# A float32 decoder trunk on one core: each 512-column product as two runs of 256 columns in one PSUM bank

## The chip, the core and the metric

The kernel runs on one core of one Trainium2 chip. The metric is the device time of one execution in microseconds; the number that counts is the median over several runs.

## The reference

One layer of a hybrid decoder on 2048 tokens of width 1024, in float32, with 16 learned tokens put in front and dropped at the end:

```
h = concat(meta, x)                                # 2064 x 1024
u = rmsnorm(h);  p = u @ w_in                      # 1024 -> 1792
y = concat(pool(p_a), conv31(p_b), rglru(p_c))     # three causal mixers
h = h + y @ w_out                                  # 1024 -> 1024
u = rmsnorm(h)
h = h + square(relu(u @ w_up)) @ w_down            # 1024 -> 4096 -> 1024
out = rmsnorm(h)[16:]
```

The four big products (w_in, w_out, w_up, w_down) are nearly all of the arithmetic. The mixers add moving averages, a depthwise convolution of 31 taps with a layer norm, a gated linear recurrence, and small products of their own.

## The kernel before

**Layout.** Activations lie channel-major, [channel, token]: 128 channels on the partitions, tokens along the columns. The tokens are worked off in four chunks of 512 (the first has the 16 extra tokens and 528 columns).

**Products.** Every float32 operand is split into a high part and the rest (`split`, lines 87 and 88: ScalarE writes the high part, VectorE the rest). A product adds hi*hi, hi*lo and lo*hi. One *item* is one block of 128 output channels for one chunk: `mm_tile` (line 178) runs over eight blocks k of 128 input channels and three split products each, that is 24 matmuls of 512 columns that add up in one PSUM bank (a tile `pm`, five of them). In the first chunk the inner projections have two sub-ranges of 264 columns in two banks, 48 matmuls an item. The instruction is recorded at line 184.

**The tiles.** The token side of a product is a list of eight split tiles [128, 2, columns]. Tiles with the tag `U` (eight of 2 x 512 columns, from `a_tile`) hold the input of later chunks' projections and the hidden values between the up and the down product. Tiles with the tag `H` (eight of 2 x 528, from `b_tile`) hold the first chunk's input, the mixers' output (for w_out) and the normed input of the up product. Weights are streamed: a DMA brings 128 x 1024 values (tag `wr`, three tiles), and two splits make two tiles `wh` of 4 blocks k each (five tiles in all). A weight block is split at most one item ahead.

**Items and their order.** They are listed by hand: W (input projection, 14 items a chunk), O (w_out, 8), U (up, 8 for each of four groups g) and D (down, 8 for each group). A chunk's mlp is U, D, U, D and so on: eight U items give the eight hidden tiles which the next eight D items read. `evac_u` (line 626) makes a hidden tile out of a U item's bank: relu and square on ScalarE (630, 632), a cast and a subtraction on VectorE (633, 634). `evac_d` adds a D item's bank to the residual (639). In the last group of the last chunk the D items are done in two halves of 256 tokens, each half with its weights streamed anew, so that the final norm of the first half can begin early.

**What runs beside them.** Behind every item `pump` issues pieces of other work (the next chunk's mixers, norms and splits) up to a budget of estimated nanoseconds; the scheduler of the language may place an instruction that is ready ahead of one that still waits, and so small matmuls of the mixers (tag `pb`) stand among those of the items.

Of the kernel before, what the change touches and what calls it, by code (L numbers as in the profile page):

```python
"""Hybrid decoder trunk: pool / conformer-conv / RG-LRU mixers and a squared-ReLU MLP on one core.

Activations are held channel-major, [channel, token], in four chunks of 512 tokens.  Every
matrix product splits both float32 operands exactly into a 12-bit high part and the 12-bit
rest, and adds the three products hi*hi, hi*lo and lo*hi in float32.
"""
# [12 lines left out]
P = 128  # L19
D = 1024  # L20
KB = D // P
NT = 512
NCH = 4
META = 16
W0 = NT + META
# [9 lines left out]
BUD1 = 2000  # L35
GELU_C = 0.7978845608028654

# packed per-channel vectors: name -> (first column, columns)
_VECS = [
    ("g1", 8), ("g2", 8), ("gf", 8), ("psc", 2), ("lam", 4), ("ba", 4), ("bx", 4),  # L40
    ("rcb", 4), ("cb", 2), ("lng", 2), ("lnb", 2), ("rcw", 16), ("cw", 62),
# [5 lines left out]
    _o += _c  # L47
NVEC = _o

# projection blocks in the order they are computed: (kind, index, weight block)  # L50
_WORDER = (
    [("bv", 0, 2), ("bg", 0, 4), ("bv", 1, 3), ("bg", 1, 5)]
    + [("cx", i, 10 + i) for i in range(4)]
# [5 lines left out]
def build(nc, tc, x0, xr, w_in, w_out, w_up, w_down, vecs, gates, pools, pws, out):  # L59
    V = nc.vector  # L60
    A = nc.scalar
    T = nc.tensor
# [24 lines left out]
        A.activation(out=hi, in_=src, func=AF.Copy)  # L87
        V.tensor_tensor(out=lo, in0=src, in1=hi.bitcast(F32), op=ALU.subtract)  # L88

# [1 line left out]
    vec = t_("vec", NVEC, 1)  # L91
    nc.sync.dma_start(out=vec, in_=vecs)

# [18 lines left out]
    def load_consts():  # L112
        for name, src, cols in (("gw", gates, 1024), ("pw", pws, 512), ("pl", pools, 256)):
            raw = t_("wr", 1024, 3)
            nc.sync.dma_start(out=raw[:, :cols], in_=src)
            hl = t_("c_" + name, (2, cols), 1, F32R)
            split(hl[:, 0, :], hl[:, 1, :], raw[:, :cols])
            cst[name] = hl
            yield 1500
        # csp = 8 * softplus(-lam)  # L120
        lam = vr("lam")
        s = t_("sp", (8, 4), 1)
        al, e, den, w, w2, q, m = (s[:, i, :] for i in range(7))
        V.tensor_scalar(out=al, in0=lam, scalar1=-1.0, scalar2=None, op0=ALU.mult)
        V.tensor_scalar(out=m, in0=al, scalar1=0.0, scalar2=None, op0=ALU.max)
        V.tensor_tensor(out=al, in0=al, in1=lam, op=ALU.max)
        A.activation(out=e, in_=al, func=AF.Exp, scale=-1.0)
        V.tensor_scalar(out=den, in0=e, scalar1=2.0, scalar2=None, op0=ALU.add)
        V.reciprocal(den, den)
        V.tensor_tensor(out=w, in0=e, in1=den, op=ALU.mult)  # L130
        V.tensor_tensor(out=w2, in0=w, in1=w, op=ALU.mult)
        NTERM = 10
        V.tensor_scalar(out=q, in0=w2, scalar1=1.0 / (2 * NTERM + 1), scalar2=1.0 / (2 * NTERM - 1), op0=ALU.mult, op1=ALU.add)
        for i in range(NTERM - 2, -1, -1):
            V.tensor_tensor(out=q, in0=q, in1=w2, op=ALU.mult)
            V.tensor_scalar(out=q, in0=q, scalar1=1.0 / (2 * i + 1), scalar2=None, op0=ALU.add)
        V.tensor_tensor(out=q, in0=q, in1=w, op=ALU.mult)
        V.scalar_tensor_tensor(out=q, in0=q, scalar=2.0, in1=m, op0=ALU.mult, op1=ALU.add)
        csp = t_("csp", (2, 4), 1)
        V.tensor_scalar(out=csp[:, 0, :], in0=q, scalar1=-8.0, scalar2=None, op0=ALU.mult)  # L140
        V.tensor_scalar(out=csp[:, 1, :], in0=q, scalar1=4.0, scalar2=None, op0=ALU.mult)
        cst["csp"] = csp
        yield 2500
# [3 lines left out]
    tail_x = [t_(f"tlx{i}", 3, 1) for i in range(4)]  # L147
    state = [t_(f"st{i}", 1, 1) for i in range(4)]

# [1 line left out]
    class Weights:  # L151
        def __init__(self, srcs):
            self.srcs = srcs
# [22 lines left out]
                self.ns += 1  # L176

    def mm_tile(w, rhs, subs):
        """Sum over KB blocks of w-block^T @ rhs-block; rhs: list of [P, 2, cols] split tiles."""
        pss = [ps_main() for _ in subs]  # L180
        for k in range(KB):
            for j, (a, b) in enumerate(((0, 0), (0, 1), (1, 0))):
                for ps, (s0, s1) in zip(pss, subs):
                    T.matmul(  # L184
                        ps[:, : s1 - s0], w[k // 4][:, a, (k % 4) * P : (k % 4 + 1) * P], rhs[k][:, b, s0:s1],
                        start=(k == 0 and j == 0), stop=(k == KB - 1 and j == 2),
                    )
        return pss

    def mm3(ps, pairs, first=True, last=True):  # L190
        """ps = sum of split products; pairs: (w hi, w lo, rhs hi, rhs lo)."""
        n = len(pairs)
        for q, (wh, wl, rh, rl) in enumerate(pairs):
            T.matmul(ps, wh, rh, start=(first and q == 0), stop=False)  # L194
            T.matmul(ps, wh, rl, start=False, stop=False)  # L195
            T.matmul(ps, wl, rh, start=False, stop=(last and q == n - 1))  # L196
# [6 lines left out]
        return hi, lo  # L203

    def colsum(src):
        """Sum over the partitions, on every partition."""
        n = src.shape[-1]
        hi, lo = split_new(src)
        ps = ps_back()
        T.matmul(ps[:, :n], ones, hi, start=True, stop=False)  # L210
        T.matmul(ps[:, :n], ones, lo, start=False, stop=True)  # L211
        return ps

    def rsqrt_of(pss, bounds, scale):
        """1/sqrt(scale * ps + eps)"""
        rs = t_("rs", W0, 2)
        for ps, (c0, c1) in zip(pss, bounds):
            A.activation(out=rs[:, c0:c1], in_=ps[:, : c1 - c0], func=AF.Sqrt, bias=eps, scale=scale)  # L218
        c0, c1 = bounds[0][0], bounds[-1][1]
        V.reciprocal(rs[:, c0:c1], rs[:, c0:c1])  # L220
        return rs
# [6 lines left out]
            A.activation(out=sq[:, c0:c1], in_=src, func=AF.Square)  # L228
            V.tensor_tensor(out=ss[:, c0:c1], in0=ss[:, c0:c1], in1=sq[:, c0:c1], op=ALU.add)  # L229

# [1 line left out]
    class Chunk:  # L232
        pass

# [21 lines left out]
        return t_("H", (2, W0), 8, F32R)  # L256

    def gen_x0(o):
        """The first chunk: gain and split, then 1/rms with its sums over channels on the tensor engine."""
        o.x = []  # L260
        tw = o.tw
        raws = []
        for k in range(KB):
            raw = t_("xr", W0, 3) if k < 3 else t_("t", W0, TB)
            nc.sync.dma_start(out=raw, in_=x0[k])
            raws.append(raw)
            if k == 0:
                wts.dma(1)
        for k in range(KB):
            hl = b_tile()  # L270
            if k == 0:
                wts.split(1)
            A.activation(out=hl[:, 0, :], in_=raws[k], func=AF.Copy, scale=vc("g1", k))
            V.scalar_tensor_tensor(out=hl[:, 1, :], in0=raws[k], scalar=vc("g1", k), in1=hl[:, 0, :].bitcast(F32), op0=ALU.mult, op1=ALU.subtract)
            o.x.append(hl)
        yield 0
        pss = [ps_back() for _ in subs_of(o)]
        for k in range(KB):
            sq = t_("m", W0, 2)
            A.activation(out=sq, in_=raws[k], func=AF.Square)  # L280
            for ps, (s0, s1) in zip(pss, subs_of(o)):
                T.matmul(ps[:, : s1 - s0], ones.bitcast(F32), sq[:, s0:s1], start=(k == 0), stop=(k == KB - 1))  # L282
        o.rs1 = rsqrt_of(pss, subs_of(o), 1.0 / D)
        yield 0

    def gen_x(o):
        """A later chunk: gain, split and, except for the second, 1/rms."""
        o.x = []
        if o.c > 1:
            ss = t_("ss", W0, 2)  # L290
# [12 lines left out]
            yield 3500  # L303

    def gen_late(o):
        """1/rms of a chunk whose projections were stored as they came, and their scaling by it."""
        ss = t_("ss", W0, 2)
        for k in range(KB):
            raw = t_("xr", W0, 3)
# [73 lines left out]
                V.tensor_copy(tail_a[i], t[:, NT:W0])  # L383
            o.done.add(("ua", i))

# [1 line left out]
    def gen_pool(o, b):  # L387
        u = o.ua[b]
        lo_half, up_half = slice(0, 64), slice(64, 128)
        # s2[:, j] = u[j] + u[j-1], s4 the sum of four, and so on  # L390
        s2 = t_("s", W0, SBF)
        V.tensor_tensor(out=s2[:, 1:W0], in0=u[:, 1:W0], in1=u[:, 0 : W0 - 1], op=ALU.add)
        yield 620
# [65 lines left out]
    def gen_rg(o, i):  # L459
# [18 lines left out]
        yield 620  # L478
        csp = cst["csp"]
        a = t_("t", W0, TB)  # L480
        # a = exp(-x), s = tanh(x/2): 1 - a = (1 + a) s, sqrt(1 - a^2) = (1 + a) sqrt(s)
        A.activation(out=a[:, R], in_=r[:, R], func=AF.Exp, scale=csp[:, 0, i : i + 1])
        s = r
        A.activation(out=s[:, R], in_=r[:, R], func=AF.Tanh, scale=csp[:, 1, i : i + 1])
# [33 lines left out]
        yield 670  # L518

    class Lane:  # L520
        """Generators run one after the other, each as soon as what it reads is there."""

        def __init__(self, todo):
            self.todo = todo
# [20 lines left out]
    class Mix:  # L545
# [17 lines left out]
            self.turn = 0  # L563

        def step(self):
            """One piece of work; None when nothing is ready."""
            pat = PAT0 if self.o.c == 0 else PAT1
            want = pat[self.turn % len(pat)]
            if not self.lanes[-1].empty() and self.o.c == 1:
# [24 lines left out]
            o.u[k] = hl  # L594
            yield 620

# [1 line left out]
    def htile(o, j):  # L598
        if o.c == NCH - 1 and j >= 4:
            return t_("Pcx", 531, 4)  # L600
# [50 lines left out]
            nc.sync.dma_start(out=out[o.c, k, :, s0:s1], in_=h)  # L651
            yield 660

# [1 line left out]
    urgent = []  # L655
    mixes = []

# [144 lines left out]


def _blockdiag(w):
    """[heads, 64, 64] -> [128, heads/2, 128], two heads on each diagonal, zeros elsewhere."""
    n = w.shape[0] // 2
    r = np.zeros((P, n, P), w.dtype)
    for i in range(n):
        r[:64, i, :64] = w[2 * i]
        r[64:, i, 64:] = w[2 * i + 1]  # L810
    return r
# [60 lines left out]
```

## Time and profile before

| | |
|---|---|
| median of 3 runs | 2005.9 us (2004.64, 2005.90, 2006.65) |
| profiled execution, first to last instruction | 2002.8 us |
| TensorE matmuls | busy 1983.2 us (99%), 8952 instructions |
| TensorE weight loads | busy 1615.8 us (81%), 8952 instructions |
| VectorE | busy 1305.1 us (65%) |
| ScalarE | busy 925.4 us (46%) |
| HBM | 104 GB/s over the span |

For the profiled execution the span is its own time: no other figure of it is given, and what lies between span and device time (start and end) is only seen as the distance to the runs. Matmul rows overlap their neighbours, so busy time says little of the pace; the distance from start to start does.

### The profile page before, as it was taken

How to read it: one execution, taken by the hardware profiler on the slowest of the kernel's cores; microseconds unless marked ns; L12 is line 12 of the kernel's file. 1: busy time of each engine (PE TensorE's matmuls, PEld its weight loads, DVE VectorE, ACT ScalarE, POOL GpSimd, SP SyncE). 2: the span in 40 equal slices, each digit the busy share in tenths (PEclk: the TensorE clock that was granted, in tenths of full speed). 3: DMA queues.
4: the chain of work that ended last, by engine and by line, in shares of the span. 5: the costliest groups of instructions: out<-in, count | busy, mean ns of one | idle time of the engine just before them, and what ended most of it. 6: DMA issues, size and time to landing. Idle time of an engine off the chain costs nothing.

```text
span 2002.8 us, 23381 instructions
## 1 busy us (share of the span) xinstructions
PE 1983.2 (99%) x8952; PEld 1615.8 (81%) x8952; DVE 1305.1 (65%) x2092; ACT 925.4 (46%) x1510; POOL 0.2 (0%) x4
## 2 busy tenths in 40 slices
PE   8999999999999999999999999999999999999997
PEld 8987888888887788888888778888888888888887
DVE  8985799746458996555445999645635484343447
ACT  6755544654445436446343544634624343323244
POOL 0000000000000000000000000000000000000000
PEclk9999999999999999999999999999999999999999
DMA  6113432222226222222223622222222333222234
GB/s 216 43 43 104 142 102 95 95 85 95 85 94 221 95 95 85 95 95 84 95 86 104 211 95 94 85 95 95 82 97 95 121 107 125 94 95 94 94 97 148
DMA packets 66065, 209.15 MB, mean 104 GB/s; under 512 B 7456, under 2 KB 9632, under 8 KB 65952
## 3 DMA queue, kind: packets, MB, share of 16 engines
q1 hardware_dynamic: 65952, 207.65, 31.7%
q8 instruction: 70, 1.15, 0.2%
q14 instruction: 43, 0.35, 0.1%
HBM read 199.23 MB, written 8.39 MB: 104 GB/s over the span
## 4 chain that ended last, share of the span: by engine, by line
PE 95%; DVE 3%; ACT 1%; DMA 1%; issue 0%; SPq 0%; DVEq 0%; ACTq 0%
PE pm L184 92%; PE pb L194 1%; PE pb L195 1%; DVE h L650 1%; PE pb L196 1%; DMA xr<-d_xr 1%; DVE wh L88 1%; DVE rs L220 1%; PE pb L282 0%; DVE ss L229 0%; PE pb L210 0%; DMA xr<-d_x 0%; PE pb L211 0%; DVE h L610 0%; DVE Pcx L650 0%
## 5 line engine op out<-in xcount | busy, mean ns | idle before, releaser
L184 PE MATMUL pm<-H,wh 128*128 128x512 f32 (+1 forms) x4416 | 983.7, 382 | 6.3 <-ACT wh L87 6.2
L184 PE MATMUL pm<-U,wh 128*128 128x512 f32 (+1 forms) x4272 | 961.7, 384 | 0.7 <-DVE wh L88 0.7
L184 PEld LDWEIGHTS pm<-H,wh 128*128 128x128 f32 x4416 | 800.0, 188 | 179.4 <-ACT wh L87 6.2
L184 PEld LDWEIGHTS pm<-U,wh 128*128 128x128 f32 x4272 | 772.7, 188 | 179.1 <-DVE wh L88 1.8
L87 ACT ACTIVATE wh<-wr 128x512 fp32r<-128x512 f32 x684 | 429.9, 629 | 730.6 <-PE pm L184 716.5
L88 DVE TENSOR_TENSOR wh<-wr,wh 128x512 fp32r<-128x512 f32 x684 | 468.2, 689 | 445.8 <-ACT wh L87 444.0
L630 ACT ACTIVATE m<-pm 128x512 f32<-128x512 f32 x128 | 76.4, 597 | 226.0 <-PE pm L184 223.7
L639 DVE TENSOR_TENSOR h<-h,pm 128x512 f32<-128x512 f32 (+1 forms) x116 | 77.4, 667 | 112.1 <-PE pm L184 111.7
L424 DVE SCALAR_TENSOR_TENSOR ca<-Pbv,vec,ca 128x512 f32<-128x512 f32 x180 | 125.9, 744 | 0.1
L634 DVE TENSOR_TENSOR U<-m,U 128x512 fp32r<-128x512 f32 x128 | 88.2, 689 | 3.0
L632 ACT ACTIVATE m<-m 128x512 f32<-128x512 f32 x128 | 79.6, 622 | 0.0
L220 DVE RECIPROCAL rs<-rs 128x512 f32<-128x512 f32 (+2 forms) x17 | 53.9, 3169 | 14.4 <-ACT rs L218 14.3
L229 DVE TENSOR_TENSOR ss<-ss,m 128x512 f32<-128x512 f32 (+1 forms) x84 | 53.8, 642 | 6.3 <-ACT m L228 5.2
L633 DVE CAST U<-m 128x512 fp32r<-128x512 f32 x128 | 53.5, 418 | 0.1
L424 DVE SCALAR_TENSOR_TENSOR ca<-h,vec,ca 128x512 f32<-128x512 f32 x60 | 42.9, 745 | 0.1
L228 ACT ACTIVATE m<-h 128x512 f32<-128x512 f32 (+1 forms) x51 | 30.9, 605 | 9.4 <-DVE h L639 3.6
L610 DVE TENSOR_TENSOR h<-pm,xr 128x512 f32<-128x512 f32 x28 | 19.1, 684 | 19.8 <-PE pm L184 19.5
L466 DVE SCALAR_TENSOR_TENSOR t<-Pcx,vec,t 128x512 f32<-128x512 f32 x36 | 26.8, 744 | 0.8 <-ACT t L464 0.6
L477 ACT ACTIVATE t<-pb,vec 128x512 f32<-128x512 f32 (+1 forms) x40 | 22.3, 603 | 8.6 <-PE pb L196 8.3
L639 DVE TENSOR_TENSOR Pcx<-Pcx,pm 128x512 f32<-128x512 f32 (+1 forms) x20 | 11.6, 581 | 19.5 <-PE pm L184 19.5
L88 DVE TENSOR_TENSOR H<-s,H 128x512 fp32r<-128x512 f32 x32 | 20.9, 686 | 1.5 <-ACT H L87 1.3
L487 ACT ACT_TABLE_LOAD x16 | 20.5, 1283 | 0.3
(183 smaller groups left out, 810.8 us busy)
## 6 DMA issues: line engine op xcount, KB each, us to landing
wr<-d_w_down SPq DMA_DIRECT2D x136, 512.0 KB, 3.5
wr<-d_w_up SPq DMA_DIRECT2D x128, 512.0 KB, 3.5
wr<-d_w_in SPq DMA_DIRECT2D x46, 512.0 KB, 3.6
wr<-d_w_out SPq DMA_DIRECT2D x32, 512.0 KB, 3.5
xr<-d_xr SPq DMA_DIRECT2D x56, 256.0 KB, 3.3
d_out<-h SPq DMA_DIRECT2D x24, 256.0 KB, 3.0
xr<-d_x SPq DMA_DIRECT2D x8, 256.0 KB, 3.0
t<-d_x SPq DMA_DIRECT2D x5, 264.0 KB, 5.8
```

What stands on the lines that cost most here:

```text
L87: A.activation(out=hi, in_=src, func=AF.Copy)
L88: V.tensor_tensor(out=lo, in0=src, in1=hi.bitcast(F32), op=ALU.subtract)
L184: T.matmul(ps[:, : s1 - s0], w[k // 4][:, a, (k % 4) * P : (k % 4 + 1) * P], rhs[k][:, b, s0:s1], start=(k == 0 and j == 0), stop=(k == KB ...
L220: V.reciprocal(rs[:, c0:c1], rs[:, c0:c1])
L228: A.activation(out=sq[:, c0:c1], in_=src, func=AF.Square)
L229: V.tensor_tensor(out=ss[:, c0:c1], in0=ss[:, c0:c1], in1=sq[:, c0:c1], op=ALU.add)
L424: V.scalar_tensor_tensor(out=a, in0=o.ub[i][:, k : k + NT], scalar=vc("cw", i * CONVK + k), in1=a, op0=ALU.mult, op1=ALU.add)
L630: A.activation(out=r, in_=ps, func=AF.Relu)
L632: A.activation(out=r, in_=r, func=AF.Square)
L633: V.tensor_copy(hl[:, 0, :], r)
L634: V.tensor_tensor(out=hl[:, 1, :], in0=r, in1=hl[:, 0, :].bitcast(F32), op=ALU.subtract)
L639: V.tensor_tensor(out=h, in0=h, in1=ps[:, : s1 - s0], op=ALU.add)
```

## The change

`mm_tile` gets a second way for items with one sub-range, which is all but the two-bank items of the first chunk. It cuts the columns in pieces of 256 and does all 24 matmuls of the first piece, then all 24 of the second. The two pieces lie side by side in the same PSUM tile, so it is read out once, by the same instructions as before, when both are complete. An item of 512 columns has 48 matmuls and 48 weight loads; an item of 256 columns (the halves at the end) has one piece and is as it was. Nothing else is changed; the rest of the diff takes comments out.

```diff
+HALF = 256
...
     def mm_tile(w, rhs, subs):
         pss = [ps_main() for _ in subs]
+
+        def mm(ps, d0, k, a, b, s0, s1, j):
+            T.matmul(
+                ps[:, d0 : d0 + s1 - s0], w[k // 4][:, a, (k % 4) * P : (k % 4 + 1) * P], rhs[k][:, b, s0:s1],
+                start=(k == 0 and j == 0), stop=(k == KB - 1 and j == 2),
+            )
+
+        prods = ((0, 0), (0, 1), (1, 0))
+        if len(subs) == 1:
+            (ps,), ((s0, s1),) = pss, subs
+            for h0 in range(s0, s1, HALF):
+                for k in range(KB):
+                    for j, (a, b) in enumerate(prods):
+                        mm(ps, h0 - s0, k, a, b, h0, min(h0 + HALF, s1), j)
+            return pss
         for k in range(KB):
-            for j, (a, b) in enumerate(((0, 0), (0, 1), (1, 0))):
+            for j, (a, b) in enumerate(prods):
                 for ps, (s0, s1) in zip(pss, subs):
-                    T.matmul(
-                        ps[:, : s1 - s0], w[k // 4][:, a, (k % 4) * P : (k % 4 + 1) * P], rhs[k][:, b, s0:s1],
-                        start=(k == 0 and j == 0), stop=(k == KB - 1 and j == 2),
-                    )
+                    mm(ps, 0, k, a, b, s0, s1, j)
         return pss
```

## The prediction

> **What bounds the kernel now.** I read the page first: engines, chain, costliest groups.
>
> ```profile
> span 2002.8 us, 23381 instructions
> PE 1983.2 (99%) x8952; PEld 1615.8 (81%) x8952; DVE 1305.1 (65%) x2092; ACT 925.4 (46%) x1510; POOL 0.2 (0%) x4
> PE 95%; DVE 3%; ACT 1%; DMA 1%; issue 0%; SPq 0%; DVEq 0%; ACTq 0%
> L87 ACT ACTIVATE wh<-wr 128x512 fp32r<-128x512 f32 x684 | 429.9, 629 | 730.6 <-PE pm L184 716.5
> ```
>
> TensorE is the chain: 95% of the end is matmul time, and it hardly ever stands still. So the question is what one matmul costs in the stream. "Mean ns of one" cannot say that, because neighbouring matmuls overlap; the starts can. The second view groups the matmuls of the big products by shape, and gives the counts:
>
> ```profile
> L184 PE MATMUL pm<-H,wh 128*128 128x512 f32 x3936 | 919.2, 393 | 0.0
> L184 PE MATMUL pm<-U,wh 128*128 128x512 f32 x3888 | 916.9, 395 | 0.5 <-DVE wh L88 0.5
> L184 PE MATMUL pm<-H,wh 128*128 128x264 f32 x480 | 64.5, 290 | 6.3 <-ACT wh L87 6.2
> L184 PE MATMUL pm<-U,wh 128*128 128x256 f32 x384 | 44.8, 277 | 0.2 <-DVE wh L88 0.2
> ```
>
> The last row matters most: the last group of down products of the last chunk is already worked off in 256-column halves. The third view is TensorE's timeline (start, length, count) around it:
>
> ```profile
> 1678.40 44.96 PE L184 MATMUL pm<-U,wh 128*128 128x512 f32 x192
> 1723.20 44.53 PE L184 MATMUL pm<-H,wh 128*128 128x512 f32 x192
> 1767.57 44.95 PE L184 MATMUL pm<-U,wh 128*128 128x512 f32 x192
> 1945.90 24.74 PE L184 MATMUL pm<-U,wh 128*128 128x256 f32 x213
> 1970.65 0.39 PE L210 MATMUL pb<-hl,ones 128*128 128x256 f32 x1
> ```
>
> From start to start, a group of 192 down matmuls (token side in U tiles) takes 1723.20 - 1678.40 = 44.80 us, 233.3 ns each. A group of up matmuls (H tiles) takes 1767.57 - 1723.20 = 44.37 us, 231.1 each. The halves take 24.75 us for 213, 116.2 each with a pause inside (below). A window behind that pause shows the undisturbed rate:
>
> ```profile
> 1950.00:1970.00 20.00, 20.00 (x179) 20.00 (x178) 1.00 0.60 190
> 1880.00:1900.00 20.00, 20.00 (x87) 16.02 (x87) 1.00 0.26 90
> ```
>
> Some 177 starts lie in 20 us (179 with the ones cut at both edges): 113.3 ns each, weight load included, at the same granted clock of 1.00. Two of those are 226.7, less than one 512.
>
> **The change, part by part.** It replaces 7824 matmuls of 512 columns (3936 + 3888, first two rows above) by 15648 of 256 columns, each with its own weight load. The 480 of 264 columns (two sub-ranges) and the 384 halves stay. Of the other engines it removes and adds nothing; it moves when tiles are needed and released.
>
> *U side, 3888.* A group of 192 becomes 384 x 113.3 = 43.5 us against 44.80: 1.3 us less, 20.25 groups, **-25.9 us**. Same tile, same weights, same shape as the row at 1945.90, so this term is nearly measured.
>
> *H side, 3936.* No row has 256 columns out of H tiles. The nearest is the first chunk's 264:
>
> ```profile
> 54.51 4.03 PE L184 MATMUL pm<-H,wh 128*128 128x264 f32 x32
> 58.38 1.80 PE L184 MATMUL pm<-U,wh 128*128 128x512 f32 x7
> ```
>
> (58.38 - 54.51) / 32 = 120.9 ns. A straight line through 264 columns at 120.9 and 512 at 231.1 gives 117.3 at 256: two cost 234.6, 3.5 more than one 512. But 8 columns fewer cannot be worth 7.6 ns (120.9 to the 113.3 of U tiles) at 0.44 ns a column, unless columns count in steps. If 264 counts as 272 (whole sixteens), the line through 272 and 512 gives 113.6 at 256, which is what the U row has. So I take 113.6: 384 x 113.6 = 43.6 against 44.37, 0.75 us a group, 20.5 groups, **-15.4 us**. Ends: 113.3 (-17.4) and 117.3 (+13.8).
>
> *The last tile of a group comes too late.* Eight up products give the eight tiles that the down products consume in the order k = 0 to 7. A down product took k = 7 after 21 of 24 matmuls, 4.9 us into itself. Now its first run gets there after 21 x 113.3 = 2.38 us, and to the rest part (one matmul on) after 2.49. The halved group shows what happens; start of the down product 1945.90, ScalarE's first row is the relu of the last up product:
>
> ```profile
> 1946.10 0.60 ACT L630 ACTIVATE m<-pm 128x512 f32<-128x512 f32 x1 [2.14 <-PE pm L184]
> 1947.11 0.62 ACT L632 ACTIVATE m<-m 128x512 f32<-128x512 f32 x1
> 1947.86 0.42 DVE L633 CAST U<-m 128x512 fp32r<-128x512 f32 x1
> 1948.31 0.69 DVE L634 TENSOR_TENSOR U<-m,U 128x512 fp32r<-128x512 f32 x1
> ```
>
> The rest is there at 1949.00, 3.10 us in, 0.61 too late; the 213 matmuls above lost 24.75 - 213 x 0.1133 = 0.62. So lateness is loss, about one for one. There are 16 such places, 15 of them new. In nine of the new ones the rest lands at +3.0 to +3.1 as here: 9 x 0.62 = 5.6. In the other six VectorE has something else in between. The worst, and a typical one (the down products start at 370.01 and 1543.78):
>
> ```profile
> 370.01 5.29 PE L184 MATMUL pm<-U,wh 128*128 128x512 f32 x22
> 373.66 0.67 DVE L634 TENSOR_TENSOR U<-m,U 128x512 fp32r<-128x512 f32 x1
> 1543.78 5.52 PE L184 MATMUL pm<-U,wh 128*128 128x512 f32 x23
> 1547.00 0.68 DVE L634 TENSOR_TENSOR U<-m,U 128x512 fp32r<-128x512 f32 x1
> ```
>
> These land at +4.32 and +3.90, 1.8 and 1.4 late; I take the typical 1.4, 8.4 for six. **+14.0 us**; ends 7 (another product's matmuls put in between) and 20.
>
> *The first up product of a chunk* also meets its tiles at double speed. Only chunk 0 is tight:
>
> ```profile
> 233.02 7.32 PE L184 MATMUL pm<-H,wh 128*128 128x512 f32 x31
> 235.40 1.29 DVE L88 TENSOR_TENSOR H<-s,H 128x512 fp32r<-128x512 f32 x2
> ```
>
> The last rest lands 236.69 - 233.02 = 3.67 in, 1.2 late: **+1.2 us**.
>
> *VectorE where it is full.* A window view of three stretches:
>
> ```profile
> core 0: us, PE busy (x) PEld busy (x) DVE busy (x) ACT busy (x) POOL busy (x), PEclk, DMA share, GB/s
> 278.00:370.00 92.00, 92.00 (x397) 74.24 (x396) 88.26 (x144) 45.42 (x71) 0.00 (x0) 1.00 0.28 92
> 647.00:772.00 125.00, 124.74 (x536) 100.00 (x535) 119.79 (x198) 60.52 (x97) 0.00 (x0) 1.00 0.29 95
> 1141.00:1266.00 125.00, 124.75 (x535) 99.87 (x534) 120.71 (x191) 60.69 (x98) 0.00 (x0) 1.00 0.29 95
> ```
>
> VectorE works 96% of these 342 us. TensorE wants to give back 2%, some 7 us of them, and VectorE could follow to about 98%, which no row shows: I charge **+3 us**, a little under half (ends 0 and 7), because part of the 7 is already in the waits above.
>
> *At nothing.* A weight half is released after 36 of 48 matmuls in place of 12 of 24, a quarter of a product, 1.4 us, later. ScalarE waits for just that (716.5 us of its idle time in the L87 row), and whatever queues behind that split in ScalarE had a whole product's time; if that cover went, each product would lose up to 1.4 us, and it would be the VectorE-full stretches that show it. The token tiles of a down product are released in its second half, still before the next up product ends. PSUM tiles are read once, after both runs, as before. SP issues the same transfers; each weight tile is used up in 5.4 us, not 5.6, and in the halved group one went every 2.7. Instruction fetch nearly doubles, but at that rate the window of 1950 to 1970 has no gap. The last 57 us, with the halves and the final norm, stay.
>
> *Sum.* -25.9 - 15.4 + 14.0 + 1.2 + 3.0 = -23.1 us on a span of 2002.8: 1979.7. The median of the runs, 2005.9, lies 3.1 above that span, so 1983 us.
>
> **The rivals.**
>
> *A fixed cost is paid twice (slower).* By the line through 264 and 512 as they stand, a matmul costs 0.444 ns a column and 3.5 ns besides, and H-side pairs cost 3.5 more than they replace: +13.8 in place of -15.4, and the sum becomes +6.1, 2012 us. The break-even is 116.5 ns for a 256 out of H tiles. For it: the only 256s seen run out of U tiles. Against it: they rule it out there, at the same clock, with loads and shape the same. The Trainium skill, "TensorE: Matmul & The Clock Gate", section "Back-to-back issue gap", gives such a rule, columns / 2.4 + 2.5 ns: 109 for 256 and 216 for 512, so that 7824 splits would cost about 20 us (an estimate by that page). The rows differ from it in size and in sign, and the U row decides for its half.
>
> *The weight loads bind.* A load's row lasts 188 ns (1615.8 us over 8952 is less only because they overlap), so two per 512 could take 376, over 1000 us more. The window of 1950 to 1970 has 178 loads in 20 us: they overlap one another. Nearly excluded.
>
> *The waits are filled.* If other products' matmuls are put into the pauses, only about 7 us of the 18.2 remain: -34, 1972 us.
>
> *VectorE keeps the gain.* If the full stretches do not shorten at all, the other 4 of the 7 us are lost, 1987; if the later release of the weights costs 0.2 us in each of their 60 products (342 / 5.6) as well, 12 more: 1999 us. For it speaks the 96%; against it that TensorE now waits 0.7 us for weights in the whole run (0.5 and 0.2 in the rows by shape).
>
> *The change does not do what it says.* Only if the pairs were not issued as whole runs; each matmul has its own load already, so nothing is shared that a run could lose.
>
> **How the numbers follow.** Forecast (1974 to 1990) 0.54; waits filled 0.14; VectorE keeps it 0.13; fixed cost on the H side 0.11, or half of it (about 1998) 0.05; something slower still, the loads among it, 0.03. About 0.2% (4 us) is what can be told from no change. The forecast, the filled waits and most of VectorE's and of the half case are faster: 0.81; the rest of those two lies within 4 us of no change: 0.05; slower 0.14. The range takes in the two cases of gain at both ends and the partial one: 1967 to 2001.
>
> **What would show it.** Up groups of 384 at 43.5 to 43.7 us and down groups at 43.5 plus 0.6 to 1.8, the excess at the 22nd and 23rd matmul. If up groups take 45 us, the H term is wrong. TensorE waits on L633/L634 would be new rows; many on L88 would be VectorE's rival.

## The result

The changed kernel takes 2042.2 us (2041.1 to 2044.4) against 2005.3 for the kernel before (2004.4 to 2006.7): ratio 1.018, 95% interval 1.017 to 1.020. It is 37 us slower; 22 us faster was forecast.

The page after, and the groups by shape:

```profile
span 2041.2 us, 39164 instructions
PE 2003.2 (98%) x16776; PEld 1983.5 (97%) x16776; DVE 1306.3 (64%) x2092; ACT 925.9 (45%) x1509; POOL 0.2 (0%) x4
PE 81%; DVE 14%; ACT 2%; issue 1%; DMA 1%; SPq 0%; DVEq 0%; ACTq 0%
L187 PE MATMUL pm<-U,wh 128*128 128x256 f32 x8160 | 955.6, 279 | 10.3 <-DVE wh L89 6.5 <-DVE U L649 3.7
L187 PE MATMUL pm<-H,wh 128*128 128x256 f32 x7872 | 942.5, 281 | 1.3 <-DVE wh L89 1.1 <-DVE H L89 0.3
```

The counts are as forecast, VectorE and ScalarE do the same work, and TensorE is still most of the chain that ended last; but VectorE has 14% of it, where it had 3%. Its timeline in the last chunk (start, length, count) answers to the groups of 192 shown before:

```profile
1712.83 44.13 PE L187 MATMUL pm<-U,wh 128*128 128x256 f32 x384
1756.81 45.60 PE L187 MATMUL pm<-H,wh 128*128 128x256 f32 x384
1802.25 45.71 PE L187 MATMUL pm<-U,wh 128*128 128x256 f32 x384
1847.79 45.61 PE L187 MATMUL pm<-H,wh 128*128 128x256 f32 x384
```

Up groups (H) take 1802.25 - 1756.81 = 45.44 us, 118.3 ns a matmul, where 44.37 stood before. Down groups (U) come in two kinds: 43.98 us, and 1847.79 - 1802.25 = 45.54 us. Before it was 44.80. Behind the pause at the eighth hidden tile all distances from start to start are 112 to 115 ns in the first kind, 113.3 on average, and 116 to 120 in the second, 117.8 on average, to the end of the group.

For the whole run I summed the distances from the start of each matmul of the big products to the start of the next matmul. "Pace" is their mean without those that a pause lengthens; the rest is "pauses".

| | before | after | change |
|---|---|---|---|
| pace, H side | 3936 x 231.4 ns | 7872 x 118.3 ns | +20.2 us |
| pace, U side, halves included | 3888 x 233.3, 384 x 113.5 | 8160 x 114.5 ns | -16.1 us |
| pauses, H and 264-column products | 4.9 us | 16.3 us | +11.4 us |
| pauses, U side | 5.9 us | 26.6 us | +20.7 us |
| small matmuls and what stands around them | 57.1 us | 59.1 us | +2.0 us |

That is +38.2 of the 38.4 us between the spans. The pauses are not all of the kind forecast. This is the timeline in the input projections of chunk 2, the third product, and the granted clock (the figure behind the busy times) before and after the gap:

```profile
675.75 4.24 PE L187 MATMUL pm<-U,wh 128*128 128x256 f32 x36
683.12 9.07 PE L187 MATMUL pm<-U,wh 128*128 128x256 f32 x54 [3.13 <-DVE wh L89]
676.00:679.00 3.00, 3.00 (x29) 3.00 (x28) 3.00 (x6) 2.62 (x5) 0.00 (x0) 1.00 0.03 5
683.00:688.00 5.00, 4.88 (x23) 4.88 (x24) 5.00 (x10) 2.95 (x4) 0.00 (x0) 0.50 0.50 152
```

TensorE waits 3.13 us for the rest part of a weight half, and then runs on at a granted clock of 0.50: matmuls of 256 columns stand 213 ns apart for the next 25. The trace's clock record has 0.50 from 682.01 to 688.84 us, and three more times in this execution for 3.41 us, before the end. In these 17.1 us the matmuls lost some 7 us of the 32 in the table (an estimate: the sum of what their distances lie above the usual ones). What VectorE did around the wait at 680:

```profile
678.59 2.07 DVE L636 SCALAR_TENSOR_TENSOR s<-h,vec,rs 128x512 f32<-128x512 f32 x3
680.58 1.88 DVE L89 TENSOR_TENSOR H<-s,H 128x512 fp32r<-128x512 f32 x3
682.39 0.68 DVE L89 TENSOR_TENSOR wh<-wr,wh 128x512 fp32r<-128x512 f32 x1
```

The weight split stands in VectorE's queue behind the norm of the chunk before. Chunk 3 shows the same, and the two projection stages, 79.6 us each before, took 83.2 and 82.1 us. Among the H products the norm's small matmuls wait for ScalarE, 6.8 us in seven waits (2.4 us in three before); one of 2.3 us is followed by half the clock as well.

### The profile page after: what moved, and what is told of

It is laid out like the page before. It is cut to its first block, busy times and chain, and to the rows that moved or that the text cites. A ratio compares the mean times of both kernels' runs of the same rounds, so it can differ in the third digit from the quotient of the medians.

```text
span 2041.2 us, 39164 instructions
## 1 busy us (share of the span) xinstructions
PE 2003.2 (98%) x16776; PEld 1983.5 (97%) x16776; DVE 1306.3 (64%) x2092; ACT 925.9 (45%) x1509; POOL 0.2 (0%) x4
## 4 chain that ended last, share of the span: by engine, by line
PE 81%; DVE 14%; ACT 2%; issue 1%; DMA 1%; SPq 0%; DVEq 0%; ACTq 0%
PE pm L187 79%; DVE ca L440 3%; DVE wh L89 2%; DVE rs L236 1%; DVE H L89 1%; DMA xr<-d_xr 1%; DVE s L636 1%; DVE h L666 1%; DVE t L482 1%; PE pb L210 1%; PE pb L211 1%; DVE ss L245 1%; PE pb L212 1%; DVE h L655 0%; ACT hl L88 0%
## 5 line engine op out<-in xcount | busy, mean ns | idle before, releaser
L187 PE MATMUL pm<-H,wh 128*128 128x256 f32 (+1 forms) x8352 | 1007.4, 282 | 7.8 <-ACT wh L88 6.4
L187 PEld LDWEIGHTS pm<-H,wh 128*128 128x128 f32 x8352 | 1000.7, 189 | 11.2 <-ACT wh L88 6.4
L187 PE MATMUL pm<-U,wh 128*128 128x256 f32 x8160 | 955.6, 279 | 10.3 <-DVE wh L89 6.5
L187 PEld LDWEIGHTS pm<-U,wh 128*128 128x128 f32 x8160 | 948.0, 189 | 17.5 <-DVE wh L89 7.2
L648 ACT ACTIVATE m<-m 128x512 f32<-128x512 f32 x128 | 79.6, 622 | 0.0
L88 ACT ACTIVATE H<-s 128x512 fp32r<-128x512 f32 x32 | 19.8, 629 | 10.7 <-DVE s L636 10.4
L311 ACT ACTIVATE U<-xr,vec 128x512 fp32r<-128x512 f32 x24 | 17.1, 717 | 14.1 <-DMA xr<-d_xr 10.6
L89 DVE TENSOR_TENSOR H<-s,H 128x512 fp32r<-128x512 f32 x32 | 20.7, 683 | 0.4 <-ACT H L88 0.4
```

Of the source, the lines that this page charges most:

```text
L187: T.matmul(ps[:, d0 : d0 + s1 - s0], w[k // 4][:, a, (k % 4) * P : (k % 4 + 1) * P], rhs[k][:, b, s0:s1], start=(k == 0 and j == 0), stop= ...
L648: A.activation(out=r, in_=r, func=AF.Square)
```

## The experiments

Times are medians, with the ratio to the kernel before where there is an interval. The theory after the result: **A**, the pace of a matmul depends on where the token part lies relative to the weight part in a partition, modulo 256 bytes, and 256 and 512 columns like different places. The compiled programs give the addresses: U tiles begin at 142560 and every 4096 bytes on, weights at 81184 and every 4096, H tiles at 47392 and every 4224, with the rest 2112 behind the high part. So U parts always lie at distance 192 from the weights (modulo 256), and H parts at 0, 64, 128 and 192 in turn. The rival, **B**: H products cost more because of a fixed cost of a matmul, wherever its operands lie.

### One side at a time

```diff
-    def mm_tile(w, rhs, subs):
+    def mm_tile(w, rhs, subs, cut=True):
...
-        if len(subs) == 1:
+        if len(subs) == 1 and cut:
```

U side only (cut is False for items that read H tiles):

> Only products that read U tiles (down products, and input projections of chunks 1 to 3) are cut into two runs of 256; those that read H tiles stay whole. By the sum of parts read from the two traces: pace on the U side 2 x 114.5 against 233.3, -16 us, and the new waits inside those products, +18 to +21: 2005 to 2011 us, 512-column H matmuls back at 231.4 ns. If the waits come from the faster pace everywhere rather than from the cut of these products, they fall to half: about 1997.

Measured: 2007.5 us (ten runs, 2002.5 to 2011.8), 1.001 (1.000 to 1.002). U 114.2 ns, H back at 231.5; pauses on the U side 25.0 us.

H side only:

> Only products that read H tiles (up products, w_out, and four of chunk 0) are cut. By the sum of parts: 7872 matmuls at 118.3 against 3936 at 231.4, +20 us, and waits +8 to +12: 2033 to 2038 us. If the 118.3 were a reaction to what the U side does, H would run near 113.5 here: about 1995.

Measured: 2033.5 us, 1.013 (1.012 to 1.015). H 118.4 ns, whatever the U side does. The surprise is in the halves at the end, which are the same code as before. Their row here:

```profile
1973.38 25.57 PE L187 MATMUL pm<-U,wh 128*128 128x256 f32 x213
1998.91 0.39 PE L226 MATMUL pb<-hl,ones 128*128 128x256 f32 x1
```

These 213 took 25.53 us, where the kernel before had 24.75: the same matmuls in the slower of the two paces. The row on which the U term was built was one of two outcomes.

### Where the token tiles lie

H tiles with every part at the same place modulo 256, 32, which is distance 0 from the weights:

```diff
-    def b_tile():
-        return t_("H", (2, W0), 8, F32R)
+    def b_tile(n=NT):
+        t = t_("H", 1088, 8, F32R)
+        return t[:, : 2 * n].rearrange("p (a b) -> p a b", a=2)
```

> The changed kernel with H tiles laid out so that every part begins at the same place modulo 256 bytes, as U tiles do (4352 bytes from tile to tile, rest 2048 behind the high part; before 4224 and 2112). Theory A (the place of the token tile's parts sets the pace): H matmuls of 256 columns fall from 118.3 to 113.3 to 117.8 ns as on the U side, mean 114.5, -30 us: about 2012 us. Theory B (a fixed cost of each matmul, whatever it reads): 118.3 stays, 2042 us.

Measured: 2045.6 us, 1.020 (1.019 to 1.022), H 119.9 ns. As it was put, theory A failed: even placing is no help. But the pace had changed, and it had become steady; so the next kernel keeps the even placing and moves the parts 48 columns on, to 224, distance 192 as on the U side.

> As the kernel with evenly placed H tiles, which all began at 32 modulo 256 bytes and took 119.9 ns steadily, but its parts begin at 224 modulo 256, where the U tiles' parts begin (weights at 32, as before). Theory A (place against the weights' place, or place alone, sets the pace): H falls to 113.3 to 117.8, mean 114.5, so -42 us against that kernel: 2003 to 2010 us. Theory B (a property of these products, or a fixed cost): 119.9 stays, 2045 us.

Measured: 2016.6 us (two runs), 1.006 (1.004 to 1.007), H 114.7 ns. The pace is the one expected under A; the time is 7 us over its range, because the pauses came to 48 us, 39 in the kernel with distance 0. Up groups of these two kernels, the first with distance 0, the second with 192:

```profile
1765.43 46.24 PE L187 MATMUL pm<-H,wh 128*128 128x256 f32 x384
1811.51 44.13 PE L187 MATMUL pm<-U,wh 128*128 128x256 f32 x384
```

```profile
1736.34 45.39 PE L187 MATMUL pm<-H,wh 128*128 128x256 f32 x384
1781.56 45.71 PE L187 MATMUL pm<-U,wh 128*128 128x256 f32 x384
```

46.08 us against 45.22, and the second is the slow one of two paces, which H now has as U does. Then the opposite: U moved by 64 bytes, to distance 0, by an unused tile of 16 columns ahead of the U tiles.

> The changed kernel with U tiles moved by 64 bytes, so that their parts begin at 32 modulo 256, as the weights do. Theory A: U matmuls of 256 columns rise from 114.5 to the 119.9 that H tiles had at that place, 8160 x 5.4 ns = +44 us: about 2086 us. Theory B: 114.5 stays, 2042 us.

Measured: 2073.7 us, 1.034 (1.032 to 1.036); U 119.9 ns as expected, while the pauses shrank by 11 us, which is why it is 2074 and not 2086. A down group:

```profile
1829.34 46.49 PE L187 MATMUL pm<-U,wh 128*128 128x256 f32 x384
1875.67 45.60 PE L187 MATMUL pm<-H,wh 128*128 128x256 f32 x384
```

It takes 46.33 us. Place alone or distance? The same unused tile ahead of everything:

> The changed kernel with everything (H, weights, U) moved by 64 bytes: U at 32, weights at 96 modulo 256, H at 96 and 224. Theory A, the distance from token part to weights counts: nothing changes, U 114.5, H 118.3, 2042 us. Theory A', the place alone counts: U 119.9, about 2086 us.

Measured: 2040.6 us, 1.018 (1.016 to 1.019); U 114.6, H 118.4, with U tiles now at the very place, 32, that had cost 119.9:

```profile
1717.37 44.13 PE L188 MATMUL pm<-U,wh 128*128 128x256 f32 x384
1761.35 45.60 PE L188 MATMUL pm<-H,wh 128*128 128x256 f32 x384
```

So it is the distance that counts, and B is out. The weights alone were never moved: that the partner is the weight tile, and not another tile that keeps its place to it, is argued from the operands of a matmul, which are just these two. Steps finer than 64 bytes were not tried.

The last two distances, H at 64 and U at 128, for the cut and for the whole products:

> The changed kernel with H at distance 64 and U at distance 128. By the few pairs seen, 120 ns at 64 and 118.2 at 128 for 256 columns: 7872 x (120 - 118.3) + 8160 x (118.2 - 114.5) = +44 us: about 2086 us. If distance 192 is not special and U products are: U stays 114.5, 2055.

Measured: 2064.8 us, one run, between the two expectations; 117.7 ns at 64 (the few pairs had said 120), 118.7 at 128. A down and an up group, 45.86 and 45.22 us:

```profile
1731.15 46.02 PE L187 MATMUL pm<-U,wh 128*128 128x256 f32 x384
1777.01 45.39 PE L187 MATMUL pm<-H,wh 128*128 128x256 f32 x384
1822.23 46.03 PE L187 MATMUL pm<-U,wh 128*128 128x256 f32 x384
```

> The kernel before with H at distance 64 and U at distance 128 from the weights. By the few pairs of such places in earlier traces H would take 232.8 and U 234.6 ns at 512 columns: 2011 to 2016 us. If only distance 0 against the rest matters: 233.3 for both, 2012.

Measured: 1997.8 us, one run, faster than both expectations; 229.7 at 64 (the few pairs seen before had said 232.8), 232.5 at 128.

### Whole products at distance 0

The kernel before, with H at distance 0:

> The kernel before (512 columns) with the evenly placed H tiles (32 modulo 256, distance 0 from the weights). If the place matters for 512 columns as for 256, twice over: 2 x (119.9 - 114.5) above the 233.3 that U has at distance 192, some 240 to 244 ns, +37 us or so: about 2042 us. If by the few pairs of such places in the trace before (231.0 ns): same as before, 2004 us.

Measured: 1989.9 us, 0.992 (0.990 to 0.994), H 227.1 ns. An up group takes 43.54 us in place of 44.37:

```profile
1711.14 43.70 PE L184 MATMUL pm<-H,wh 128*128 128x512 f32 x192
1754.68 44.96 PE L184 MATMUL pm<-U,wh 128*128 128x512 f32 x192
```

Both expectations missed: 512 columns like the place that 256 like least. And with U there too:

> The kernel before (whole products of 512), with H tiles and U tiles both at distance 0 modulo 256 from the weights. If the distance alone sets the pace of 512 columns: U falls from 233.3 to the 227.1 that H has there, 3888 x 6.2 ns = -24 us beside the -16 us of H: about 1965 us, faster than any cut kernel. If it is a property of H tiles or their products: U stays at 233.3, 1990 us.

Measured: 1967.1 us, 0.981 (0.979 to 0.982); 226.9 ns on both sides. Its groups:

```profile
1645.56 43.68 PE L184 MATMUL pm<-U,wh 128*128 128x512 f32 x192
1689.08 43.68 PE L184 MATMUL pm<-H,wh 128*128 128x512 f32 x192
1732.60 43.68 PE L184 MATMUL pm<-U,wh 128*128 128x512 f32 x192
```

43.52 us for U and H alike: 192 whole products at the right place take what 384 halves take in the faster of their paces. Nothing is cut, and no tile is needed sooner. It is the fastest kernel of the study.

### The waits

U side only, but the first down product of each group whole (`j % KB > 0` as the cut):

> As the kernel that cuts U-side products only, but the first down product of each group of eight stays whole, so that it comes to the eighth hidden tile after 4.9 us as before. If the waits at the hidden tile are lateness from the cut alone: the excess at the 21st to 26th matmul of those products vanishes, -10 to -12 us against the kernel with U side only, less 1.6 us of pace: about 1997. If VectorE's queue makes them: no change from the kernel with U side only.

Measured: 2002.7 us, 0.999 (0.998 to 1.000), against 2007.5: half of what was expected. The pauses on the U side fell from 25.0 to 14.3 us, the size that was forecast (the three down groups of the last chunk ahead of the halves take 43.7 us each), but a larger share of the groups fell into the slower pace (114.5 ns on average, not 114.2). Not all of the fall is the hidden tile: the profile of the kernel with U side only has 13.7 us at half the clock before its end, this one 3.4, which is some 4 of the 10.7 us (an estimate from the distances between matmuls in these stretches). The rest, some 7 us, is less than the 10 to 12 expected. What is left of the pauses, in the view of waits (total, times, longest):

```profile
PE pm L187 <- DVE wh L89: 7.1, 4, 3.1
```

These are mostly the projections' weight splits. The same wait in chunk 2 and in chunk 3 of this kernel, and the granted clock in the first 4 us behind it:

```profile
663.90 16.29 PE L187 MATMUL pm<-U,wh 128*128 128x256 f32 x125 [3.14 <-DVE wh L89]
1159.94 6.29 PE L187 MATMUL pm<-U,wh 128*128 128x256 f32 x53 [3.13 <-DVE wh L89]
663.90:667.90 4.00, 4.00 (x23) 4.00 (x23) 4.00 (x7) 2.95 (x4) 0.00 (x0) 0.63 0.40 131
1159.94:1163.94 4.00, 4.00 (x35) 4.00 (x36) 4.00 (x7) 3.36 (x5) 0.00 (x0) 1.00 0.42 135
```

After the first the clock falls to half from 663.41 to 666.83 us (hence the mean of 0.63), after the second, as long, it stays at 1.00. So the length of a wait does not settle it. In every trace the clock changes at whole multiples of 3.413 us from one another: in the changed kernel the half clock begins at 53.96, 651.29, 682.01 and 1187.19 us, which are 175, 9 and 148 such steps apart. Over the 18 traces, each of the 45 steps at full clock in which TensorE, by its matmul rows, stood idle for 1.95 us or more was followed by the half clock, 7 of the 23 with 1.5 to 1.95 us, and 2 of the 74 with 0.6 to 1.5 us. Of the two waits above the first has 2.65 us in one step; the second is shared between two, with 1.53 and 1.60.

Without cutting the projections:

> Only down products are cut, and the first of each group of eight stays whole; input projections, up products and w_out stay whole. By the sum of parts: 2520 products of 512 columns at 2 x 114.4 in place of 233.3, -11 us, waits +1 to +3: 1994 to 1997 us. If waits behind VectorE come with any faster pace: 2001 to 2003, as with the projections cut too.

Measured: 1994.6 us, 0.995 (0.993 to 0.996). Pauses on the U side 6.6 us, 114.4 ns. The sum of parts holds, and the cut of the projections alone had cost 8 us net. With H at distance 0 besides:

> Down products cut except the first of each group (U at distance 192, good for 256 columns), everything else whole, and H at distance 0 (good for 512 columns). If the terms add: 1994.6 - 16.5 = 1978 us. If what TensorE gains on the H side only turns into waits: 1985 or more.

Measured: 1979.4 us, 0.987 (0.985 to 0.989), H 227.1: the terms add. With the up products cut instead, H at distance 192:

> Down products and up products are cut, the first of each group of eight down products and the first up product of each chunk's four groups of eight stays whole; projections and w_out stay whole; H tiles lie as in the kernel with H at 224. By the sum of parts: against the kernel that cuts down products only (1994.6), 2944 up products or so at 2 x 114.6 in place of 231.4, -6.4 us; w_out whole at that place 233.3 in place of 231.4, +1.5; waits +1 to +3: 1990 to 1993 us. If the faster up products only move the waits behind VectorE: 1996 or more.

Measured: 2002.1 us, 0.998 (0.997 to 0.999). The pace was as expected (H 114.7, w_out whole 233.1), -4.6 us; pauses on both sides rose by some 10 us, and U had the slow pace more often, +2.6. So the up products' gain does turn into waits; some 4 of the 10 us are three stretches of 3.41 us at half the clock (an estimate as above), of which the kernel that cuts down products only has none before its end.

### What sets the floor

Pieces of 384 and 128 columns:

```diff
-HALF = 256
+HALF = 384
```

> The changed kernel with pieces of 384 and 128 columns in place of two of 256. Theory L (from 256 columns down a matmul waits for the next weight load, which needs some 113 ns, whatever is streamed): 128 columns still take 113 ns or more, 384 about 174, so 287 for 512 columns in place of 229: about 2480 us. Theory S (columns and a small fixed cost set it, the load is hidden): 128 columns 55 to 60 ns, 384 about 174: about 2030 us.

Measured: 2524.7 us, one run; the pace is that of theory L, the time 45 us above it: 384 columns 175.6 ns, 128 columns 109.5, hardly less than 256. In the timeline a pair takes 55.15 / 192 = 287 ns:

```profile
2189.63 55.31 PE L187 MATMUL pm<-H,wh 128*128 128x384 f32 x384
2244.78 55.38 PE L187 MATMUL pm<-U,wh 128*128 128x384 f32 x384
```

Something holds a matmul with its load to some 110 ns. Is it the length of the load?

```diff
+            m = P if (k, j) in ((0, 0), (KB - 1, 2)) or s1 - s0 != HALF else 64
...
-                ps[:, d0 : ...], w[k // 4][:, a, (k % 4) * P : (k % 4 + 1) * P], ...
+                ps[:m, d0 : ...], w[k // 4][:, a, (k % 4) * P : (k % 4) * P + m], ...
```

> The changed kernel, but 22 of the 24 matmuls of each run of 256 columns use only 64 of the 128 weight columns (half of the output channels are left without those products). Theory L (the load binds): with half the columns to load, the pace goes down to what 256 columns of tokens need, under 113 ns on both sides, and the place no longer matters: U and H alike. Theory S: 114.5 and 118.3 stay.

Measured: 2032.0 us, one run. The loads' rows went from 189 ns in the changed kernel to 135, and the pace stayed near what the place had made it: U 115.3 (114.5 before), H 116.7 (118.3 before).

```profile
L188 PEld LDWEIGHTS pm<-U,wh 128*64 128x64 f32 x7480 | 872.6, 135 | 20.4 <-DVE wh L89 7.3 <-DVE U L650 5.7 <-DVE U L651 4.2
```

At 256 columns the length of the load does not bind: a load shorter by 54 ns moves the pace by less than 2. What makes 128 columns cost as much as 256 was not settled.

The four distances together (ns, start to start, pauses left out):

| distance modulo 256 bytes | 256 columns | twice that | 512 columns |
|---|---|---|---|
| 0 | 119.9 | 239.8 | 226.9 |
| 64 | 117.7 | 235.4 | 229.7 |
| 128 | 118.7 | 237.4 | 232.5 |
| 192 | 113.3 or 117.8 | 226.7 or 235.6 | 233.3 |
| in turn (H as it was) | 118.3 | 236.6 | 231.4 |

Cutting gains only at distance 192, and there only in the faster pace.

## Why the prediction was wrong

**The H term was the step that failed** (-15.4 forecast, +20.2 measured). It took 113.6 ns between ends of 113.3 and 117.3 because the U row "has" 113.3, counting 264 columns as 272 to make three points fit one line. The line through the two H rows as they stood gave 117.3; measured 118.3, beyond even that end. The mistake was to let a row of U decide between two readings of H rows: that put U and H on one axis, columns, while they differed in a second thing, where the tiles lie. With H laid where U lies, H ran near U's pace, 114.7 against 114.5. The trace had a sign of it: at 512 columns H took 231.1 and U 233.3, and no term asked why.

Of the 61 us between the sum and the measured change of the span (-23.1 and +38.4), the H pace is 36, the U pace 10, the pauses 14 and the small matmuls 2.

**The U term** (-25.9, measured -16.1). The halves' row was real but one of two paces. A quarter of the U matmuls ran at 117.8, from a pause to the next disturbance. What picks the pace is not shown; it changed only at pauses and at matmuls of other shapes.

**The late eighth tile** (+14.0): right in kind, too large. The waits at the 21st to 26th matmul are there, some 9 us in the fifteen new places, 4.7 of them in chunk 0, where one grew to 3.1 us behind VectorE; in the last two chunks they cost 0.3 to 0.5 us each, because other products' matmuls are put in between, as the lower end supposed.

**VectorE where it is full** (+3, end 7): too small. The projections of chunks 2 and 3 gained 4 us of pace and lost 10 in pauses, because each had a wait of 3.1 us and here both were followed by half the clock, for 6.8 and 3.4 us. The Trainium skill, "TensorE: Matmul & The Clock Gate", section "Part 1: The HAM clock gate", says that after at least one idle window of about 3.4 us the clock falls to half. The steps of 3.413 us fit that window; that all of it has to be idle the traces do not bear out, since 1.95 us and more in one step were enough each time. The price of the half clock was in no term. That both waits were hit is in part bad luck: of the two like waits in the kernel that leaves the first down product whole, only one was.

**Chunk 0's first up product** (+1.2): 1.3 us, one wait at its second block. **At nothing**: instruction fetch did not show. TensorE's waits for ScalarE's weight splits stayed one, at the start (6.4 us, 6.2 before); whether the later release of weights had a part in the waits for VectorE's splits was not separated.

**The rivals.** "A fixed cost is paid twice" came nearest on the pace, 117.3 on the H side, and for a wrong reason: with the distance right, two matmuls of 256 take 226.7 ns in the faster pace, what one of 512 takes at its own best place (226.9). The rule of the Trainium skill, "TensorE: Matmul & The Clock Gate", section "Back-to-back issue gap", 2.5 ns more for each cut, is given there for a matmul by itself; for a stream with weight loads that section says that both set the spacing, a condition that the prediction left out. Here the rule fits only one line of the table above, distance 192 in the slower pace (2.3 more); the others go from 6.6 less to 12.9 more. "VectorE keeps the gain" named the place of the largest pauses, and priced them at 16 us or less with no loss of clock. "The waits are filled" was out: 32 us of pauses came new.

## What to carry over

Before a matmul is cut, made longer or moved, look at the distance from start to start by tile, not by shape alone; if two tiles with the same shape differ, find out why first, since that may be worth more than the change. Here 64 bytes in front of one tile and an even pitch for the other gave 1.9%, and the cut alone 0.5% at best. Work that is needed twice as soon has to be checked against every queue that makes it, and a wait of TensorE of some 2 us or more can cost more than its length, because the half clock may follow it.

## What the runs showed of the hardware

- A float32r matmul of 512 columns takes 226.9 to 233.3 ns, and one of 256 columns 113.3 to 119.9, by the distance of its token part from its weight part modulo 256 bytes; the order of the places is nearly reversed between the two sizes.
- At distance 192, 256 columns have two steady paces, 113.3 and 117.8 ns, with the same addresses, kept up for tens of microseconds until a pause.
- 128 columns take 109.5 ns, as long as 256 but for 4 to 10 ns; halving the load (189 to 135 ns) changes the pace of 256 by less than 2 ns (114.5 to 115.3, 118.3 to 116.7). Both from one run each.
- The granted clock changes at multiples of 3.413 us. It fell to half after each of 45 such steps in which TensorE was idle for 1.95 us or more, for 3.41 us or a multiple. In one execution a wait of 3.1 us with 2.65 us in one step was followed by it, and a second one, shared 1.53 and 1.60 between two steps, was not.
